# Decoder trunk with routed experts on one core: gate folded from the second quarter, one block more combined on TensorE, the scatter buffer read back in one load

## The chip, the cores and the metric

The kernel runs on one core of one Trainium2 chip. The metric is the device time of one execution in microseconds (us). The kernel before was run three times: median 2093.63 us, 2091.58 to 2093.67. One more execution was recorded by the profiler; it took 2093.2 us. Engine names are those of the profile: PE is TensorE, DVE is VectorE, ACT is ScalarE, POOL is GpSimd, SP is the engine that issues most weight loads.

## The reference

The reference is a two-layer decoder trunk on 512 tokens of width 1024, in float32. For each of four sub-layers (mixer 0, experts 0, mixer 1, experts 1) it computes

```python
h = x * (1 + scale) + shift                 # scale, shift, gate: rows made from the vector c
x = layer_norm(ALPHA * x + gate * f(h), g, b)   # ALPHA = 4 ** 0.25
```

Here f is in layer 0 a mixer of block-sparse attention and gated linear attention with one joint output projection (1024 x 1024), in layer 1 a gated delta-rule mixer with an output projection of the same size, and behind each mixer a layer of 64 experts (width 256) with one shared expert. Each token goes to 6 experts, chosen through groups; the sum is weighted by the router and scaled by 2.5.

## The kernel before, in words

**Tiles and stages.** The 512 tokens are four tiles of 128; x is kept as four tiles of 128 x 1024 floats. The span of 2091.1 us falls into layer 0's mixer (to about 381 us, with its output projection from about 283), the experts of layer 0 (to 995), layer 1's mixer (to about 1450, projection from about 1360), the experts of layer 1 (to 2065) and a tail of LayerNorm.

**Float32 by three products.** A weight slab or activation is split in a high part (ACT copies it rounded, L217) and a low part (DVE subtracts, L219), into one of two `parts` buffers; each product is three matmuls: high x high, high x low, low x high (L231, L232, L233).

**Output projection (`out_project`).** The weight is read in four quarters of 256 columns, w0 to w3, through a ring of three slots. Quarters below `FOLD` are multiplied plain, and DVE multiplies the result by the gate row `grow` (L399, into `op`) and adds it to x (L401). From `FOLD` on, POOL multiplies the weight in its slot by the gate row (L385, 128 x 2048), it is split behind that, and DVE adds PE's result directly. w0 and w1 are one step each; w2 and w3 are one step together, since the result then fills 512 columns. POOL first scales x by ALPHA (L377, four instructions). x is loaded before that.

**Rows.** A row of the gate or of LayerNorm is made by PE transposes of a broadcast column (L279) in two halves of 512 columns, which ACT copies out of PSUM (L281).

**Experts.** 64 experts stand in 38 blocks: 20 blocks of one expert, 14 of two, 4 of four. One pass of the loop, number b, holds the down projection of block b - 1 (`narrow`, L1368), gate and up projection of block b (`widen`, L1335), then transposes of the gathered tokens of block b + 1 (`turn`, L1323), two transposes of block b's hidden rows (`turn_back`, L1346), and small matmuls that find a later block's token slots (L1269). The result of a block of one is added to a buffer in DRAM, `acc`, by an indirect DMA of POOL's queue (L1375). The result of a shared block is split in `yh` and `yl` and added to x by `combine`: eight units (four token tiles, two halves), each two matmuls with a one-hot matrix into one of three `ps_tr` buffers (L1395) and one add by DVE (L1396). Behind the loop stands another loop, for experts with more tokens than their block holds; all engines meet at its head (L1711).

**Order.** In the expert loop PE's order is the order of the program. Elsewhere, and for the other engines, a scheduler orders each engine's instructions when the program is built; each engine then runs its own list in order.

## Time and profile before

| | |
|---|---|
| median of three runs | 2093.63 us |
| the profiled execution | 2093.2 us, span 2091.1 us |
| mean granted TensorE clock | 0.971 |
| PE busy | 1935.5 us, 93% |
| DVE busy | 1234.7 us, 59% |
| ACT, POOL busy | 507.1 us, 24%; 453.8 us, 22% |

The span is the time from the first to the last instruction that the profile shows. The busy time of PE is that of its matmuls; weight loads run beside them. A row of a timeline gives start, length, engine, line, operation, what it writes and reads; in brackets, the idle time of that engine just before it and what ended it. Rows of equal instructions in a run stand as one with x and their count.

### The profile page before, as it was taken

What the parts mean: (1) busy time and instruction counts of PE and PEld (TensorE: products, weight loads), DVE (VectorE), ACT (ScalarE), POOL (GpSimd) and SP (SyncE); (2) the same over time, 40 slices, a digit from 0 to 9 for tenths busy, and PEclk for the clock granted to TensorE, in tenths of its full rate; (3) what the DMA queues carried; (4) which work ended last, traced back from release to release, by engine and by line L of the source; (5) the groups of instructions that cost most, each with busy time, mean ns of one, the idle gap of its engine ahead of it and who ended that gap; (6) DMA issues with size and microseconds to landing.
All of it is one profiled execution on the core that took longest, in us unless ns stands there. A gap on an engine that the chain in (4) does not pass through costs nothing. (4 is left out here: it accounts for less than half of the span.)

```text
span 2091.1 us, 28643 instructions
## 1 busy us (share of the span) xinstructions
PE 1935.5 (93%) x10619; PEld 1189.4 (57%) x10619; DVE 1234.7 (59%) x3165; ACT 507.1 (24%) x969; POOL 453.8 (22%) x317
## 2 busy tenths in 40 slices
PE   5999879999999999998888999989999999999995
PEld 3877779644444444543676877888544444444442
DVE  6676887743553544535768877578453544544436
ACT  3412443111111111111434556423111111111111
POOL 2331234311011110111125344154211110110102
PEclk9999999999999999999889999999999999999997
DMA  8765665898998998988322112128898989989994
GB/s 308 274 235 206 219 215 212 299 362 318 411 386 330 401 353 345 400 338 320 114 72 81 41 42 67 42 106 313 323 353 345 397 312 406 371 331 399 396 359 143
DMA packets 128678, 572.17 MB, mean 274 GB/s; under 512 B 16943, under 2 KB 54255, under 8 KB 72473
## 3 DMA queue, kind: packets, MB, share of 16 engines
q1 hardware_dynamic: 103600, 499.81, 60.8%
q0 software_dynamic: 19632, 55.79, 9.5%
q10 hardware_dynamic: 5304, 14.72, 1.9%
q8 instruction: 85, 1.39, 0.3%
q14 instruction: 57, 0.46, 0.1%
HBM read 550.33 MB, written 34.61 MB: 280 GB/s over the span
## 5 line engine op out<-in xcount | busy, mean ns | idle before, releaser
L1335 PE MATMUL ps_mm<-wslot,xT 128*64 128x512 f32 (+2 forms) x1216 | 404.5, 596 | 1.2 <-ACT xT L1324 0.8
L1368 PE MATMUL ps_mm<-wslot,hT 128*64 128x512 f32 (+2 forms) x1024 | 312.8, 610 | 0.2
L1335 PE MATMUL ps_mm<-parts,xT 128*64 128x512 f32 (+2 forms) x832 | 280.0, 596 | 0.7 <-issue 0.4
L1335 PEld LDWEIGHTS ps_mm<-wslot,xT 128*64 128x64 f32 (+2 forms) x1216 | 142.1, 148 | 219.1 <-issue 205.4
L1337 DVE SCALAR_TENSOR_TENSOR hh<-hh,t,ps_mm 128x256 f32<-128x256 f32 x76 | 36.5, 480 | 360.2 <-ACT hh L1336 360.1
L1293 POOL DMA_INDIRECT xg<-hd,idx x76 | 93.5, 1230 | 579.6 <-PE ps_tr L1395 497.0
L231 PE MATMUL ps_mm<-parts,hTh 128*128 128x256 f32 x704 | 208.9, 298 | 9.4 <-DVE op L399 5.3
L1368 PEld LDWEIGHTS ps_mm<-wslot,hT 128*64 128x64 f32 (+2 forms) x1024 | 103.1, 149 | 189.9 <-issue 179.9
L232 PE MATMUL ps_mm<-parts,hTh 128*128 128x256 f32 x704 | 204.1, 291 | 0.7 <-DVE parts L219 0.4
L233 PE MATMUL ps_mm<-parts,hTl 128*128 128x256 f32 x704 | 203.5, 291 | 0.4 <-DVE hTl L1773 0.4
L1396 DVE TENSOR_TENSOR x<-x,ps_tr 128x512 f32<-128x512 f32 x288 | 183.6, 681 | 5.8 <-PE ps_tr L1395 5.1
L224 POOL TENSOR_TENSOR parts<-wslot,parts 128x512 fp32r<-128x512 f32 (+1 forms) x79 | 140.9, 1809 | 194.6 <-ACT parts L217 194.6
L1336 ACT ACTIVATE hh<-ps_mm 128x256 f32<-128x256 f32 x76 | 29.1, 383 | 619.9 <-PE ps_mm L1335 619.9
L1375 POOL DMA_INDIRECT acc<-yh,row x40 | 64.9, 1622 | 489.4 <-DVE yh L1374 480.0
L1335 PEld LDWEIGHTS ps_mm<-parts,xT 128*64 128x64 f32 (+2 forms) x832 | 93.7, 144 | 130.4 <-issue 123.2
L1395 PE MATMUL ps_tr<-yh,ohs 128*128 128x512 f32 x288 | 137.7, 478 | 26.2 <-DVEq L1711 14.1
L231 PEld LDWEIGHTS ps_mm<-parts,hTh 128*128 128x128 f32 x704 | 138.5, 197 | 13.0 <-DVE op L399 3.2
L1324 ACT ACTIVATE xT<-ps_tr 128x512 f32<-128x512 f32 x152 | 84.0, 597 | 245.7 <-PE ps_tr L1323 245.7
L232 PEld LDWEIGHTS ps_mm<-parts,hTh 128*128 128x128 f32 x704 | 138.3, 197 | 3.3 <-issue 1.3
L233 PEld LDWEIGHTS ps_mm<-parts,hTl 128*128 128x128 f32 x704 | 137.5, 196 | 1.7 <-DVE hTl L1773 0.6
L255 DVE SCALAR_TENSOR_TENSOR acc<-wslot,cact,acc 128x2048 f32<-128x2048 f32 x38 | 122.7, 3230 | 13.6 <-DMA wslot<-in_ada_w_dram 13.2
L231 PE MATMUL ps_mm<-hTh,parts 128*128 128x512 f32 (+1 forms) x296 | 124.2, 419 | 4.8 <-ACT parts L217 2.5
(457 smaller groups left out, 3114.9 us busy)
## 6 DMA issues: line engine op xcount, KB each, us to landing
wslot<-in_moe_w_down_dram SPq DMA_DIRECT2D x128, 1024.0 KB
wslot<-in_moe_w_gate_dram SPq DMA_DIRECT2D x76, 1024.0 KB
wslot<-in_moe_w_up_dram SPq DMA_DIRECT2D x76, 1024.0 KB
parts<-in_moe_w_gate_dram SPq DMA_DIRECT2D x52, 1024.0 KB
parts<-in_moe_w_up_dram SPq DMA_DIRECT2D x52, 1024.0 KB
wslot<-in_ada_w_dram SPq DMA_DIRECT2D x44, 1024.0 KB
wslot<-in_od_w_in_dram SPq DMA_DIRECT2D x16, 1024.0 KB
wslot<-in_ev_w_in_dram SPq DMA_DIRECT2D x12, 1024.0 KB
```

The lines of the kernel that those rows point to most:

```text
L224: eng.tensor_sub(lo[:, ks], v[:, ks], hi[:, ks].bitcast(F32))
L231: self.nc.tensor.matmul(out, ah, bh, start=(i == 0), stop=False)
L232: self.nc.tensor.matmul(out, ah, bl, start=False, stop=False)
L233: self.nc.tensor.matmul(out, al, bh, start=False, stop=(i == n - 1))
L255: nc.vector.scalar_tensor_tensor(acc, w, self.cact[:, k:k + 1], acc, op0=OP.mult, op1=OP.add)
L1293: self.nc.gpsimd.indirect_dma_start(out=xg, out_offset=None, in_=M["hd"], in_offset=bass.IndirectOffsetOnAxis(ap=idx, axis=0), bounds_chec ...
L1324: nc.scalar.activation(xT[:, 4 * g:4 * g + 4], pt.rearrange("p (k c) -> p k c", k=4), AF.Copy)
L1335: nc.tensor.matmul(pv[a:a + n], xT[:, i, a:a + n], w[0][:, :, i], start=(i == 0), stop=(i == KT - 1))
L1368: nc.tensor.matmul(py[a:a + n], hT[:, k, a:a + n], w[1][:, k, 512 * h:512 * h + 512], start=(k == 0), stop=(k == 1))
L1375: nc.gpsimd.indirect_dma_start(out=M["acc"], out_offset=bass.IndirectOffsetOnAxis(ap=G["tok"], axis=0), in_=yf, in_offset=None, bounds_che ...
L1395: nc.tensor.matmul(po, G["oh"][:, t], y[:, cs], start=(i + k == 0), stop=(i == len(Gs) - 1 and k == 1))
L1396: nc.vector.tensor_add(self.x[t][:, cs], self.x[t][:, cs], po)
```

## The change

- `FOLD` goes from 2 to 1: the gate is folded in the weights of w1, w2 and w3, in both layers.
- In layer 0's mixer the second half of the gate row and of the two LayerNorm rows is copied out of PSUM by DVE (`both`).
- A block of one is added to `acc` only if it is not among the last four blocks (`stored`). This concerns block 35, which now goes through `combine` at iteration 36.
- `acc` is read back by one DMA of 2 MB at iteration 35, into a slot of the expert weights, and added to x by four POOL instructions at iteration 36. Before, eight DMAs of 256 KB and eight DVE adds stood at iteration 37 (L1636, L1637).
- In an iteration with `combine`, all eight units stand behind turn, slots and turn_back. Before, four stood ahead of them and four behind.
- The second half of `route_extra`, which makes the table of the extra experts, moves from iteration 4 to iteration 5.

```diff
--- before.py
+++ after.py
@@ -34,7 +34,7 @@
 NX = 1
 EARLY = 4
 LEAD = 3
-FOLD = 2
+FOLD = 1
 LANES = 64
 ALPHA = float(4 ** 0.25)
 LN_EPS = 1e-5
@@ -68,6 +68,13 @@
 
 
 BLOCKS = blocks()
+
+
+def stored(b):
+
+    return len(BLOCKS[b]) == 1 and b < len(BLOCKS) - 4
+
+
 SPE = (mybir.EngineType.SP,)
 
 
@@ -270,7 +277,7 @@
             nc.vector.tensor_add(m, m, b)
         return end
 
-    def row(self, out, col, scale=1.0):
+    def row(self, out, col, scale=1.0, both=False):
 
         for h in range(2):
             pt = self.ptile("tr")
@@ -278,7 +285,10 @@
                 kk = 4 * h + k
                 self.nc.tensor.transpose(pt[:, k * P:(k + 1) * P], col[:, kk:kk + 1].to_broadcast([P, P]),
                                          self.ident)
-            self.nc.scalar.activation(out[:, h * 512:(h + 1) * 512], pt, AF.Copy, scale=scale)
+            if both and h:
+                self.nc.vector.tensor_copy(out[:, h * 512:(h + 1) * 512], pt)
+            else:
+                self.nc.scalar.activation(out[:, h * 512:(h + 1) * 512], pt, AF.Copy, scale=scale)
 
     def rows_here(self, new, which, l, scale=1.0):
 
@@ -288,7 +298,7 @@
             self.row(t[k], self.lncol[:, 2 * which + k, l, :], scale)
         return t
 
-    def rows_next(self, new, which, l, nxt):
+    def rows_next(self, new, which, l, nxt, both=False):
 
         nc = self.nc
         g, b = self.lncol[:, 2 * which, l, :], self.lncol[:, 2 * which + 1, l, :]
@@ -300,7 +310,7 @@
         t = []
         for k in range(2):
             t.append(new("lnrow"))
-            self.row(t[k], cg[:, k])
+            self.row(t[k], cg[:, k], both=both)
         return t
 
     def ln_stats(self, x):
@@ -1238,6 +1248,7 @@
         nc.vector.tensor_scalar(oh[:, 2], ex[:, :E], xcol, -1.0, op0=OP.subtract, op1=OP.mult)
         nc.vector.scalar_tensor_tensor(oh[:, 2], oh[:, 2], 1.0, oh[:, 0], op0=OP.add, op1=OP.mult)
         nc.vector.tensor_reduce(lst, oh[:, 1:3], axis=X, op=OP.add)
+        yield
         pl = self.ptile("sm")
         for k in range(2):
             nc.tensor.matmul(pl[:, L * k:L * k + L], lst[:, k:k + 1].to_broadcast([L, P]),
@@ -1496,8 +1507,8 @@
         def slots():
 
             if nsl[0] < NB:
-                b = BLOCKS[nsl[0]]
-                g = self.slots_of(M, M["posm"], M["vals"], [x[0] for x in b], len(b) == 1)
+                b = nsl[0]
+                g = self.slots_of(M, M["posm"], M["vals"], [x[0] for x in BLOCKS[b]], stored(b))
                 nsl[0] += 1
                 yield next(g)
                 at.append(next(g))
@@ -1532,7 +1543,7 @@
 
             for b in range(NB + 1):
                 n = len(BLOCKS[b - 1]) if b > SINGLE else 0
-                first = n if n == 2 else n // 2
+                first = n if n == 2 or n == 1 and not stored(b - 1) else n // 2
                 yield from down(b - 1, range(first))
                 if b < NB:
                     yield from wide(b)
@@ -1598,7 +1609,7 @@
                     else:
                         fetch(total)
                     if b < NB:
-                        G[b]["w"], G[b]["one"] = W[b], len(W[b]) == 1
+                        G[b]["w"], G[b]["one"] = W[b], stored(b)
                         row.append(self.widen(M, G[b]))
                     if not todo:
                         row.reverse()
@@ -1610,31 +1621,29 @@
                     if todo and b < NB:
                         units = [lambda g=todo, t=t, h=h: self.combine(g, t, h) for t in range(TT) for h in range(2)]
                         todo = []
-                    for u in units[:4]:
-                        u()
                     if b + 1 < NB:
                         ahead()
                     if b < NB and not units:
                         self.turn_back(M, G[b])
                     if b + 1 < NB:
                         self.turn(M, G[b + 1])
+                    next(sl, None)
                     if b < NB and units:
                         self.turn_back(M, G[b])
-                    next(sl, None)
-                    for u in units[4:]:
+                    for u in units:
                         u()
                     units = []
                     if b == NB - 3 and pre:
                         pre(False)
                     if b == NB - 1 and pre:
                         pre(True)
-                    if b == NB - 1:
+                    if b == NB - 3:
+
+                        back = self.eslot(M).rearrange("p (t d) -> p t d", t=TT)
+                        nc.gpsimd.dma_start(back, M["acc"][:S].rearrange("(t p) d -> p t d", p=P))
+                    if b == NB - 2:
                         for t in range(TT):
-                            for h in range(2):
-                                cs = slice(512 * h, 512 * h + 512)
-                                y = self.wk("acc")
-                                nc.gpsimd.dma_start(y, M["acc"][t * P:(t + 1) * P, cs])
-                                nc.vector.tensor_add(self.x[t][:, cs], self.x[t][:, cs], y)
+                            nc.gpsimd.tensor_add(self.x[t], self.x[t], back[:, t])
                     if b == NB - 8:
                         wds = [wd[:, 1], wd[:, 0]]
                         new = lambda n: wds.pop()
@@ -1643,7 +1652,11 @@
                         for t in range(TT):
                             self.ln_here(self.x[t], M["mv"][t], here, nc.vector, nc.vector)
                     if b == 4:
-                        self.route_extra(M)
+                        rest = self.route_extra(M)
+                        next(rest)
+                    if b == 5:
+                        for _ in rest:
+                            pass
                         for k in range(2):
                             nc.vector.tensor_mul(wd[:, k], wd[:, k], grow)
                     if 8 <= b < 24 and b % 2 == 0:
@@ -1826,8 +1839,8 @@
             grow = new("grow")
             while len(todo) > 2:
                 fill(1)
-            self.row(grow, self.mod[:, 0, 2])
-            rows = self.rows_next(new, 0, 0, (self.mod[:, 0, 3], self.mod[:, 0, 4]))
+            self.row(grow, self.mod[:, 0, 2], both=True)
+            rows = self.rows_next(new, 0, 0, (self.mod[:, 0, 3], self.mod[:, 0, 4]), True)
             wr = self.router(0, new)
             self.out_project(mixed, d["ev_w_out"][0], grow, d["x"][0], fill, (0, 1, 4, 5, 6, 7, 2, 3))
             while todo or queue:
```

Lines below the change move: L385 becomes L395, L399 and L401 become L409 and L411, L219 and L217 become L226 and L224, L231 to L233 become L238 to L240, L1335 and L1368 become L1346 and L1379, L1395 becomes L1406, L1230 and L1243 become L1240 and L1254, L1323 becomes L1334, L1346 (turn_back) becomes L1357, L1269 becomes L1280.

On DVE, in layer 1's output projection, the list before reads so from the split of w2 (L219, first row) to the first sum of w2 and w3 (last row); the split of w1 stands 12 rows ahead of the first gate multiply and is not in the piece.

```order
L219 TENSOR_TENSOR parts<-wslot,parts 128x2048
L399 TENSOR_TENSOR op<-ps_mm,grow 128x256
L401 TENSOR_TENSOR x<-x,op 128x256
L311 BN_STATS bn<-x 128x6
L399 TENSOR_TENSOR op<-ps_mm,grow 128x256
L401 TENSOR_TENSOR x<-x,op 128x256
L311 BN_STATS bn<-x 128x6
L399 TENSOR_TENSOR op<-ps_mm,grow 128x256
L401 TENSOR_TENSOR x<-x,op 128x256
L311 BN_STATS bn<-x 128x6
L219 TENSOR_TENSOR parts<-wslot,parts 128x2048
L401 TENSOR_TENSOR x<-x,ps_mm 128x512
```

The same place now, from the splits of w1 and w2 (L226 x2) on:

```order
L226 TENSOR_TENSOR parts<-wslot,parts 128x2048 x2
L411 TENSOR_TENSOR x<-x,ps_mm 128x256
L321 BN_STATS bn<-x 128x6
L411 TENSOR_TENSOR x<-x,ps_mm 128x256
L321 BN_STATS bn<-x 128x6
L411 TENSOR_TENSOR x<-x,ps_mm 128x256
L321 BN_STATS bn<-x 128x6
L411 TENSOR_TENSOR x<-x,ps_mm 128x256
L321 BN_STATS bn<-x 128x6
L226 TENSOR_TENSOR parts<-wslot,parts 128x2048
L411 TENSOR_TENSOR x<-x,ps_mm 128x512
```

The split of w1 moved to behind quarter 0's adds, next to that of w2, and the four gate multiplies of quarter 1 (L399) are gone. On POOL the four scalings of x (L387) are followed by three gatings (L395) where there were two, and on ACT the three splits (L224) stand in one run.

On PE, in iteration 4 of the first expert loop, the table of the extra experts (L1230, L1231, L1243) stands so ahead of the down projection (L1368):

```order
L1230 LDWEIGHTS rx
L1230 MATMUL ps_sm<-supper_b,rx 64x64
L1231 LDWEIGHTS rx
L1231 MATMUL ps_sm<-upper_b,rx 64x64
L1243 MATMUL ps_sm<-call,rx 128x64 x2
L1368 MATMUL ps_mm<-wslot,hT 64x512 x8
```

and now:

```order
L1240 LDWEIGHTS rx
L1240 MATMUL ps_sm<-supper_b,rx 64x64
L1241 LDWEIGHTS rx
L1241 MATMUL ps_sm<-upper_b,rx 64x64
L1379 MATMUL ps_mm<-wslot,hT 64x512 x8
```

The two matmuls L1243 (now L1254) went to iteration 5, behind the combine.

On PE, in iteration 5, from the last of widen (first row), before:

```order
L1335 MATMUL ps_mm<-wslot_3688,xT 128x512 x8
L1395 MATMUL ps_tr<-yh,ohs 128x512
L1395 MATMUL ps_tr<-yl,ohs 128x512
L1395 MATMUL ps_tr<-yh,ohs 128x512
L1395 MATMUL ps_tr<-yl,ohs 128x512
L1395 MATMUL ps_tr<-yh,ohs 128x512
L1395 MATMUL ps_tr<-yl,ohs 128x512
L1395 MATMUL ps_tr<-yh,ohs 128x512
L1395 MATMUL ps_tr<-yl,ohs 128x512
L1323 MATMUL ps_tr<-call,xg_2910 128x128 x8
L1346 MATMUL ps_sm<-call,hh 128x128 x2
```

and now:

```order
L1346 MATMUL ps_mm<-wslot_3681,xT 128x512 x8
L1334 MATMUL ps_tr<-call,xg_2903 128x128 x8
L1280 LDWEIGHTS oh
L1280 MATMUL ps_sm<-tb,oh 128x5
L1280 LDWEIGHTS oh
L1280 MATMUL ps_sm<-tb,oh 128x5
L1280 LDWEIGHTS oh
L1280 MATMUL ps_sm<-tb,oh 128x5
L1280 LDWEIGHTS oh
L1280 MATMUL ps_sm<-tb,oh 128x5
L1357 MATMUL ps_sm<-call,hh 128x128 x2
L1406 MATMUL ps_tr<-yh,ohs 128x512
```

All units (L1406) begin behind turn (L1334), the slots (L1280) and turn_back (L1357).

## Rows read from the trace of the kernel before

**Rows 1.** The profile page, part 1: busy time of each engine (us, share, instructions).

```profile
PE 1935.5 (93%) x10619; PEld 1189.4 (57%) x10619; DVE 1234.7 (59%) x3165; ACT 507.1 (24%) x969; POOL 453.8 (22%) x317
```

**Rows 2.** What TensorE waited for: us in total, times, longest.

```profile
PE ps_tr L1395 <- DVEq L1711: 14.1, 2, 8.0
PE ps_tr L1395 <- DVE x L1396: 12.1, 30, 4.0
...
PE ps_mm L231 <- DVE op L399: 5.3, 2, 3.0
PE ps_sm L1243 <- DVE rx L1240: 4.6, 2, 2.3
```

**Rows 3.** Timeline of POOL, layer 1's out_project: start us, us, instruction [idle before <-releaser].

```profile
1369.08 9.37 POOL L385 TENSOR_TENSOR wslot<-wslot,grow 128x2048 f32<-128x2048 f32 x2
```

**Rows 4.** Timeline of ACT, the same stretch.

```profile
1373.72 1.92 ACT L217 ACTIVATE parts<-wslot 128x2048 fp32r<-128x2048 f32 x1 [13.48 <-POOL wslot L385]
1379.84 1.91 ACT L217 ACTIVATE parts<-wslot 128x2048 fp32r<-128x2048 f32 x1 [4.19 <-PE ps_mm L233]
```

**Rows 5.** Timeline of DVE, the same stretch.

```profile
1368.52 0.42 DVE L399 TENSOR_TENSOR op<-ps_mm,grow 128x256 f32<-128x256 f32 x1 [0.31 <-PE ps_mm L233]
1369.15 4.82 DVE L401 TENSOR_TENSOR x<-x,op 128x256 f32<-128x256 f32 x1 [0.21 <-POOL x L377]
...
1379.38 2.27 DVE L219 TENSOR_TENSOR parts<-wslot,parts 128x2048 fp32r<-128x2048 f32 x1
...
1391.46 0.69 DVE L401 TENSOR_TENSOR x<-x,ps_mm 128x512 f32<-128x512 f32 x1 [3.07 <-PE ps_mm L233]
```

**Rows 6.** Timeline of POOL, layer 0's out_project.

```profile
293.58 11.17 POOL L385 TENSOR_TENSOR wslot<-wslot,grow 128x2048 f32<-128x2048 f32 x2
```

**Rows 7.** Timeline of DVE, layer 0's out_project.

```profile
293.65 6.69 DVE L255 SCALAR_TENSOR_TENSOR acc<-wslot,cact,acc 128x2048 f32<-128x2048 f32 x1 [2.07 <-DMA wslot<-in_ada_w_dram]
...
320.38 0.69 DVE L401 TENSOR_TENSOR x<-x,ps_mm 128x512 f32<-128x512 f32 x1 [2.43 <-PE ps_mm L233]
```

**Rows 8.** Timeline of ACT, layer 0's out_project.

```profile
309.32 1.91 ACT L217 ACTIVATE parts<-wslot 128x2048 fp32r<-128x2048 f32 x1 [9.19 <-PE ps_mm L233]
```

**Rows 9.** Timeline of PE, iteration 4 of the first expert loop.

```profile
445.42 1.11 PE L1243 MATMUL ps_sm<-call,rx 64*128 64x64 f32 x4 [2.29 <-DVE rx L1240]
446.47 5.32 PE L1368 MATMUL ps_mm<-wslot,hT 128*64 128x512 f32 x16
```

**Rows 10.** A window around that row: PE PEld DVE ACT POOL busy, PEclk, DMA share, GB/s.

```profile
446.00:452.00 6.00, 6.00 (x20) 2.05 (x20) 1.72 (x5) 0.63 (x1) 0.08 (x1) 0.68 0.75 221
```

**Rows 11.** Timeline of PE, an iteration with a block of two experts.

```profile
558.27 0.40 PE L1395 MATMUL ps_tr<-yh,ohs 128*128 128x512 f32 x1
...
558.74 0.39 PE L1395 MATMUL ps_tr<-yh,ohs 128*128 128x512 f32 x1
...
559.56 0.50 PE L1395 MATMUL ps_tr<-yh,ohs 128*128 128x512 f32 x1 [0.20 <-DVE x L1396]
```

**Rows 12.** Timeline of DVE, the same iteration.

```profile
558.82 2.48 DVE L1396 TENSOR_TENSOR x<-x,ps_tr 128x512 f32<-128x512 f32 x4
```

**Rows 13.** Timeline of PE, an iteration with a block of four.

```profile
660.95 0.50 PE L1395 MATMUL ps_tr<-yl,ohs 128*128 128x512 f32 x1 [0.98 <-DVE yl L1384]
```

**Rows 14.** Timeline of PE, the end of the first expert loop.

```profile
978.18 0.50 PE L1395 MATMUL ps_tr<-yh,ohs 128*128 128x512 f32 x1
...
983.22 3.65 PE L1368 MATMUL ps_mm<-wslot,hT 128*64 128x512 f32 x16
994.90 0.80 PE L1395 MATMUL ps_tr<-yh,ohs 128*128 128x512 f32 x1 [8.02 <-DVEq L1711]
```

**Rows 15.** Timeline of DVE, the end of the first expert loop.

```profile
986.42 3.09 DVE L1637 TENSOR_TENSOR x<-x,acc 128x512 f32<-128x512 f32 x5
...
993.19 0.68 DVE L1382 TENSOR_TENSOR y<-ps_mm,grow 128x512 f32<-128x512 f32 x1
```

**Rows 16.** DMA issues: KB each, us to landing.

```profile
acc<-xg POOLq DMA_DIRECT2D x2, 2560.0 KB, 16.0
```

## Prediction

> **What bounds the kernel now.** Read part 1 of the page first: TensorE (PE) is busy in 93% of the span [rows 1]. So a change can pay only by shortening PE's waits, by letting PE run at its full clock, or by giving PE less to do. The second view is the list of what PE waited for. The change touches these rows of it: 14.1 us for VectorE (DVE) to reach the loop behind the experts, 12.1 us for the adds of the combine, 5.3 us for the gate multiply of the output projection, 4.6 us for the extra experts' table; the waits on yl are read from a timeline [rows 2, 13]. Together the four are near 36 us, less than 2% of the span. The rest of the views are timelines of the stretches where those waits stand: the output projection of each mixer, one iteration of the expert loop for each kind of block, and the loop's end.
>
> The sum is made against the profiled execution, 2093.2 us (span 2091.1); the median of the runs is 2093.63.
>
> **1. Gate folded from the second quarter: layer 1.** Before, quarter 1 (w1) was split early, so PE ran it straight behind quarter 0: quarter 0's last result came at 1368.5, and ScalarE (ACT) got w1's buffer back at 1379.8, so quarter 1 took 11.3 us [rows 4, 5]. POOL gated w2 and w3 in that shadow, from 1369.1, 4.7 us each [rows 3]. Now w1 itself stands at the head of that queue, behind the same four scalings of x, and ACT's split of it behind the gating: 1369.1 + 4.7 = 1373.8, + 1.9 for ACT [rows 4] = 1375.7. Then DVE must make the low half, 2.27 us alone [rows 5]. But DVE's add with both operands in SBUF took 4.82 us beside the gating, and ended when POOL's instruction did [rows 3, 5]; the multiply of the same size ahead of it took 0.42. So I let DVE's split of w1 wait for POOL's second instruction, till 1378.5, and end at 1380.7. PE stands idle from 1368.5: 12.2 us with nothing to cover it, where it had none. Quarter 1 then runs till 1392.0, and at half clock at first. A long wait before costs about 1.7: behind a 2.29 us wait the same 16 matmuls took 5.32 instead of 3.65, at a mean granted clock of 0.68, a mix of the levels 1.2 and 2.4 GHz [rows 9, 10, 14]. That gives 1393.7. w3 needs w1's buffer, so it is split behind that (1.9 + 2.3, 1397.9), hidden by two tiles of w2 (48 of quarter 1's 96 matmuls, 5.6 us, till 1399.3). The first sum lands 2.9 us later, at 1402.2; before it landed at 1391.5 [rows 5]: +10.7. The gate wait of the last row (5.3 - 3.0 = 2.3 us, [rows 2]) is gone within this. Off goes what the early split of w1 no longer takes from ACT and DVE ahead of the projection, at most 1.9 (ACT's copy). I take **+8.5**. Bounds: DVE not held up (-2.8), no half clock (-1.7): +4; a gating of quarter 1 held up in its turn by DVE: +12.
>
> The Trainium skill ("SBUF — State Buffer", section "SBUF: two separate sides") says that DVE with two SBUF inputs and a reading GpSimd take a shared port pair as an exclusive lock, held for the whole instruction, not as a split of bandwidth. The 4.82 agrees. With a split of bandwidth the low half of w1 would be done at about 1378 to 1379, and the sum would fall by about 2 per layer.
>
> **2. The same in layer 0.** POOL gates from 293.6, 11.17/2 = 5.6 us an instruction with DVE against it, 4.7 without [rows 6]. w1 is gated at 298.2, split by ACT at 300.1, by DVE behind w2's gating at about 305. Before, quarter 1 ended at 309.3 [rows 8], in spite of a 3.0 us wait in its middle, for DVE was held by a modulation step of 6.69 us [rows 2, 7]; that wait goes, since that step now stands behind the splits. Quarter 1 now ends at 305 + 11.3 + 1.7 = 318, which is +8.7. The last two modulation slabs are loaded only when w1's and w2's slots are free (305 and 309.6): they are worked off just before 318, so they are hidden, and cost up to 4 if that cover fails. The halves of the LayerNorm rows copied by DVE are 3 copies of about 0.7 (as the last DVE row of [rows 5], the same size) behind its scaling of mixed, and ACT's three copies less and one split less bring the rows 1 to 2 earlier. I take **+6.5** for the layer; bounds +3 to +10.
>
> **3. The extra experts' table in two halves.** The second half moves to iteration 5, behind the combine. Twice PE waited 2.3 for it [rows 2, 9]; and the half-clock matmuls behind it go. 2 x (2.3 + 1.7) = **-8**. Bounds -4.6 (the clock falls elsewhere) to -8.5. DVE has a whole iteration for those steps, about 16 us (983.2 - 446.5 over 33 iterations, [rows 9, 14]), so nothing is late next.
>
> **4. Eight combine units in one piece.** Of the 18 shared blocks per layer, four are fours. There PE waits 0.98 for yl [rows 13]; turn, slots and turn_back now stand ahead and cover it, but the later adds bunch up: -0.4 each, **-3** in all. For the 14 twos, the two groups of four with a rest between become eight in a row. DVE's adds come every 0.62 (2.48/4, [rows 12]), PE's units, undisturbed, every 0.47 (558.27 to 558.74, [rows 11]), and there are three ps_tr buffers: unit 8 cannot begin before add 5 is done. Before, the same iteration lost 0.20 in one wait [rows 11]. Now: add 1 starts 0.6 behind unit 1, five adds take 3.1, so unit 8 begins 3.7 behind unit 1 where PE alone wants 3.3: 0.4 lost, 0.1 to 0.2 more than before. 28 of these, 0.15 each: **+4**; bounds -7 to +7, for DVE's small copies may fall on either side of the adds.
>
> **5. Block 35 combined, the buffer back in one load.** Iteration 36 gets eight units more, 5.0 us in the last iteration, 978.18 to 983.22 [rows 14]: +4.5 per layer, PE time with no cover. What goes: eight DVE adds, 8 x 0.62, which stand between narrow's end and the last scaling of y (986.4 to 993.2, [rows 15]), and the waits on eight loads among them. PE waited 8.0 and 6.1 there [rows 2, 14]. Without the adds the y scaling follows narrow's end at once, and what is left is ACT's and DVE's split and the loop's entry, some 3 us: 5 and 3 off. Net about **+1** for both layers; bounds -4 to +5. The load of 2 MB is bounded by the 2.5 MB load's 16.0 us [rows 16] and is issued in iteration 35; POOL's four adds of about 2.4 each follow, and the next combine that needs x stands one iteration later. So both are hidden, by about 3 us; a load slower by 5 would show as 2 us per layer.
>
> By the page named above, a DVE add that takes one operand from PSUM is not held by that lock, so POOL's four adds would not slow the combine beside them; no run so far shows that pair. If they did, up to 4 x 2.4 per layer would come on top.
>
> **Sum:** 8.5 + 6.5 - 8 - 3 + 4 + 1 = +9, that is 2102.2 against the profiled run, 2102.6 against the median.
>
> **The rivals.**
> *Gains win (faster, about 2086).* Quarter 1 is late by less than the waits it removes. POOL's gating of w1 starts sooner, or DVE's split gets between POOL's instructions: with the low bounds of terms 1 and 2 (+4, +3), the waits on the loop's entry falling to 2 each (-10 in place of -8 in term 5, so -1), -8, -4, and 0 for the twos: -6 to -8. For it: the early split of w1 also cost ACT and DVE time ahead of the projection, and no row shows three gatings in a row. Against: POOL's queue has the scalings first, and the one row of DVE beside a gating is a full wait. Chance 0.24.
> *No change (about 2093).* Terms 1 and 2 at +5 each, the rest as summed to -6, -3 for twos that gain instead of lose. Chance 0.17.
> *A larger loss (about 2112).* The place is the end of both loops. If the load back comes later than the next combine, POOL's adds hold DVE's, and those PE's units: from 3 us of lateness on, each us counts in both layers; with terms 1 and 2 at their upper bounds (+22) and this at +3, the sum is +18 to +20. Chance 0.15; the forecast itself 0.44.
>
> **Chances.** A measurement of this kernel can't tell 0.2% (4.2 us) from no change. Slower by more: the forecast and the larger loss, 0.59. Same 0.17, faster 0.24. The range for 8 in 10: 2086 to 2114. The forecast's own is 2097 to 2108.
>
> **What would show it.** Right: in layer 1 PE idle for 10 us or more ahead of quarter 1, ended by DVE's split of w1, and that split's start or its length tied to the end of POOL's second gating; the first sum of quarters 2 and 3 8 to 11 us later behind the last of quarter 0; no wait on rx, and full clock in iteration 4; the wait for the loop's entry down to about 3. Wrong: quarter 1 starting less than 5 us behind quarter 0, the twos' iterations shorter than before by over 0.2 us, or PE waiting on x in the last combine.

## The result, and the profile after

The changed kernel took 2110.06 us (median of 3 runs, 2106.03 to 2112.76) against 2093.63; the ratio is 1.0076, with an interval of 1.0059 to 1.0094, that is 12 to 20 us slower. Its profiled execution took 2112.76 us, with a span of 2110.8, the longest of its three runs: what follows explains 19.7 us of span, not the 16 of the medians.

Where they came from is read from the same PE instruction in both timelines, the first transposes for a block of the expert loop (L1323 before, L1334 after). The shift of its start, after minus before:

| stretch | shift at its end, us | of which here |
|---|---|---|
| layer 0's mixer, to the transposes for block 0 | 7.8 | +7.8 |
| experts of layer 0, to the transposes for block 37 | 8.6 | +0.8 |
| last iterations, second loop, layer 1's mixer | 17.7 | +9.1 |
| experts of layer 1, to the transposes for block 37 | 17.6 | -0.1 |
| last iterations, second loop, tail | 19.7 | +2.0 |

These are single executions. Of the +7.8 of the first row, up to 2.9 can be chance: e3_route below, which changes nothing ahead of that point, is 2.9 us late there too.

The waits of PE after (total us, times, longest) show the trade. PE's old rows on op and on rx [rows 2] are gone, the wait for the second loop fell from 14.1 to 5.1; new on top stand the two halves of a split weight:

```profile
PE ps_mm L238 <- ACT parts L224: 17.1, 3, 7.4
...
PE ps_mm L239 <- DVE parts L226: 8.0, 3, 3.9
PE ps_tr L1406 <- DVE x L1407: 8.0, 5, 3.5
...
PE ps_tr L1406 <- DVEq L1724: 5.1, 2, 2.9
```

**The projection of layer 1.** POOL's timeline after, which answers to [rows 3], has three gatings in a row:

```profile
1376.93 15.71 POOL L395 TENSOR_TENSOR wslot<-wslot,grow 128x2048 f32<-128x2048 f32 x3
```

ACT's, against [rows 4]; the splits of w1, w2 and w3:

```profile
1381.45 1.91 ACT L224 ACTIVATE parts<-wslot 128x2048 fp32r<-128x2048 f32 x1 [13.63 <-POOL wslot L395]
1386.11 1.91 ACT L224 ACTIVATE parts<-wslot 128x2048 fp32r<-128x2048 f32 x1 [2.75 <-POOL wslot L395]
1401.81 1.92 ACT L224 ACTIVATE parts<-wslot 128x2048 fp32r<-128x2048 f32 x1 [13.79 <-PE ps_mm L240]
```

DVE's, against [rows 5]: quarter 0's last multiply and add, the low halves of w1 and w2 in one row, the first sum of w2 and w3:

```profile
1376.10 0.42 DVE L409 TENSOR_TENSOR op<-ps_mm,grow 128x256 f32<-128x256 f32 x1
1376.99 4.71 DVE L411 TENSOR_TENSOR x<-x,op 128x256 f32<-128x256 f32 x1 [0.47 <-POOL x L387]
1383.39 11.40 DVE L226 TENSOR_TENSOR parts<-wslot,parts 128x2048 fp32r<-128x2048 f32 x2 [1.69 <-ACT parts L224]
...
1409.11 0.69 DVE L411 TENSOR_TENSOR x<-x,ps_mm 128x512 f32<-128x512 f32 x1 [3.06 <-PE ps_mm L240]
```

And PE's, from the stretch where it had one wait of 2.4 us before:

```profile
1383.41 1.01 PE L238 MATMUL ps_mm<-parts,hTh 128*128 128x256 f32 x3 [7.35 <-ACT parts L224]
1388.28 0.58 PE L239 MATMUL ps_mm<-parts,hTh 128*128 128x256 f32 x1 [3.86 <-DVE parts L226]
```

ACT copies w1 as soon as POOL has gated it (1381.45), PE begins quarter 1 with the high half (wait of 7.35) and stops after three matmuls for the low half (3.86). Quarter 1 then starts at the lower level of the clock: the granted clock was 0.50 in 1388 to 1393 us and 0.99 in 1393 to 1399. DVE's row of 11.40 us is two instructions of 2.27: the first ends at 1388.2, behind POOL's second gating (1376.93 + 2 x 4.6 = 1386.1) by its own length, the second behind the third gating. From quarter 0's last multiply to the first sum of the last two quarters it is now 33.0 us (1376.10 to 1409.11); before it was 22.9 (1368.52 to 1391.46).

**The experts.** In iteration 4 the wait on rx is gone in both layers, but in layer 0 the matmuls behind it still run at half clock in part (5.35 us, as long as with the wait), against [rows 9, 10]; PE's timeline, and a window with the granted clock in the third number from the end:

```profile
450.85 5.35 PE L1379 MATMUL ps_mm<-wslot,hT 128*64 128x512 f32 x16
```

```profile
450.00:456.00 6.00, 5.93 (x22) 1.95 (x22) 4.64 (x27) 0.63 (x1) 1.45 (x2) 0.72 1.02 360
```

So layer 0 gained 2.6 us there, layer 1 5.3. An iteration with a block of four, against [rows 13], from the yh that the first unit waits for to the next iteration's first matmuls:

```profile
668.96 0.51 PE L1406 MATMUL ps_tr<-yh,ohs 128*128 128x512 f32 x1 [0.39 <-ACT yh L1394]
669.68 0.50 PE L1406 MATMUL ps_tr<-yl,ohs 128*128 128x512 f32 x1 [0.22 <-DVE yl L1395]
...
674.78 1.51 PE L1346 MATMUL ps_mm<-wslot,xT 128*64 128x512 f32 x6
```

and DVE in it:

```profile
670.93 0.68 DVE L1407 TENSOR_TENSOR x<-x,ps_tr 128x512 f32<-128x512 f32 x1
...
671.59 4.26 DVE L1407 TENSOR_TENSOR x<-x,ps_tr 128x512 f32<-128x512 f32 x7
```

Eight adds follow each other, from 670.93 to 675.8, and PE has only units to run beside them: 0.61 us longer in this iteration than before. For a block of two the difference is 0.02. Behind the transposes for block 13, in both layers, another row is new: the granted clock was 0.57 in 584 to 588 us, a mix of its two levels, and the down projection there took 4.18 us, where 3.63 is usual:

```profile
583.43 3.08 PE L1457 MATMUL ps_mm<-wd,sh 128*128 128x512 f32 x4
586.44 4.18 PE L1379 MATMUL ps_mm<-wslot,hT 128*64 128x512 f32 x16
```

That cost 1.65 us in each layer. A third stretch of the kind, 1.6 us, stands behind the transposes for block 31 of layer 1 (granted clock 0.66 in 1959 to 1964 us): sixteen transposes took 3.23 us for 1.97 before, and the row behind them, 3.65 before, took 3.99:

```profile
1962.40 3.99 PE L1379 MATMUL ps_mm<-wslot,hT 128*64 128x512 f32 x16
```

Ahead of all three PE had run sixteen small matmuls of the slots (128 x 5) with waits under 0.3 us. The kernel before has the same run ahead of its full-clock row behind block 31, so these matmuls alone do not decide it.

**The end of the loop.** DVE and PE, against [rows 14, 15]:

```profile
982.12 6.02 DVE L1397 TENSOR_SCALAR ohs<-call,t 128x128 fp32r<-128x128 f32 x3
```

```profile
992.65 0.50 PE L1357 MATMUL ps_sm<-call,hh 128*128 128x128 f32 x2 [1.00 <-DVE hh L1348]
...
1004.06 1.33 PE L1406 MATMUL ps_tr<-yh,ohs 128*128 128x512 f32 x2 [2.87 <-DVEq L1724]
```

PE's wait for the second loop fell from 8.02 to 2.87 us in layer 0, which pays for the eight units there. DVE's three one-hot tiles, 0.67 us in the iteration before, took 6.02, since POOL was adding (978.70 to 988.05). The load itself landed in time:

```profile
wslot<-acc POOLq DMA_DIRECT2D x2, 2048.0 KB, 19.4
```

### The profile page after: what moved, and what is told of

It is laid out like the page before. It is cut to its first block, busy times and chain, and to the rows that moved or that the text cites. A ratio compares the mean times of both kernels' runs of the same rounds, so it can differ in the third digit from the quotient of the medians.

```text
span 2110.8 us, 28677 instructions
## 1 busy us (share of the span) xinstructions
PE 1955.9 (93%) x10651; PEld 1189.3 (56%) x10651; DVE 1250.1 (59%) x3170; ACT 507.9 (24%) x971; POOL 474.8 (22%) x311
## 5 line engine op out<-in xcount | busy, mean ns | idle before, releaser
L1346 PE MATMUL ps_mm<-wslot,xT 128*64 128x512 f32 (+2 forms) x1216 | 404.5, 596 | 1.2 <-ACT xT L1335 1.0
L1379 PE MATMUL ps_mm<-wslot,hT 128*64 128x512 f32 (+2 forms) x1024 | 311.0, 606 | 0.1
L1346 PE MATMUL ps_mm<-parts,xT 128*64 128x512 f32 (+2 forms) x832 | 279.9, 596 | 1.0 <-ACT xT L1335 0.7
L1346 PEld LDWEIGHTS ps_mm<-wslot,xT 128*64 128x64 f32 (+2 forms) x1216 | 142.1, 148 | 219.8 <-issue 205.4
L238 PE MATMUL ps_mm<-parts,hTh 128*128 128x256 f32 x704 | 207.8, 298 | 17.6 <-ACT parts L224 14.6
L1379 PEld LDWEIGHTS ps_mm<-wslot,hT 128*64 128x64 f32 (+2 forms) x1024 | 102.6, 148 | 189.4 <-issue 178.3
L240 PE MATMUL ps_mm<-parts,hTl 128*128 128x256 f32 x704 | 203.5, 291 | 0.0
L231 POOL TENSOR_TENSOR parts<-wslot,parts 128x512 fp32r<-128x512 f32 (+1 forms) x79 | 141.3, 1815 | 195.8 <-ACT parts L224 185.5
L1346 PEld LDWEIGHTS ps_mm<-parts,xT 128*64 128x64 f32 (+2 forms) x832 | 92.8, 144 | 131.0 <-issue 122.7
L1406 PE MATMUL ps_tr<-yh,ohs 128*128 128x512 f32 x304 | 146.1, 482 | 17.0 <-DVE x L1407 8.0
L238 PEld LDWEIGHTS ps_mm<-parts,hTh 128*128 128x128 f32 x704 | 138.0, 197 | 21.3 <-ACT parts L224 15.0
L240 PEld LDWEIGHTS ps_mm<-parts,hTl 128*128 128x128 f32 x704 | 137.9, 197 | 1.0 <-DVE hTl L361 0.2
L1335 ACT ACTIVATE xT<-ps_tr 128x512 f32<-128x512 f32 x152 | 83.4, 595 | 188.0 <-PE ps_tr L1334 185.3
L1406 PE MATMUL ps_tr<-yl,ohs 128*128 128x512 f32 x304 | 124.7, 412 | 3.6 <-DVE yl L1395 3.6
L238 PE MATMUL ps_mm<-hTh,parts 128*128 128x512 f32 (+1 forms) x296 | 123.4, 417 | 4.8 <-ACT parts L224 2.5
```

The source lines that it names most:

```text
L231: eng.tensor_sub(lo[:, ks], v[:, ks], hi[:, ks].bitcast(F32))
L238: self.nc.tensor.matmul(out, ah, bh, start=(i == 0), stop=False)
L240: self.nc.tensor.matmul(out, al, bh, start=False, stop=(i == n - 1))
L1335: nc.scalar.activation(xT[:, 4 * g:4 * g + 4], pt.rearrange("p (k c) -> p k c", k=4), AF.Copy)
L1346: nc.tensor.matmul(pv[a:a + n], xT[:, i, a:a + n], w[0][:, :, i], start=(i == 0), stop=(i == KT - 1))
L1379: nc.tensor.matmul(py[a:a + n], hT[:, k, a:a + n], w[1][:, k, 512 * h:512 * h + 512], start=(k == 0), stop=(k == 1))
```

## The experiments

Each kernel was run in five rounds beside the kernel before; differences in us are worked out from the ratio of the runs times 2094.

**e1_fold2.** The changed kernel with one line back:

```diff
-FOLD = 1
+FOLD = 2
```

> The changed kernel with FOLD = 2 again; all its other parts stay. Theory (the fold costs about 8 us in each projection, for quarter 1 waits for gating, split and the lock between POOL and DVE): the two waits of 7.3 and 3.9 us ahead of quarter 1 go in both layers, and the time falls by 16 us against the changed kernel, to about +0 to +4 against the kernel before. Rival (the loss is made in the expert loop, by the combine in one piece and the load back; the projection's waits are made good later): the time falls by less than 5 us, and the kernel stays above +11 against before.

Measured: ratio 1.0006 (0.9997 to 1.0016), +1 us against before, 15 less than the changed kernel. The fold carries the loss: in its profile the two waits on the halves of w1 are gone in both layers.

**e2_fold1.** The kernel before with the opposite edit.

> The kernel before with FOLD = 1 and nothing else. Theory: +16 us (7.8 in layer 0, 8.2 in layer 1), with the waits ahead of quarter 1 as in the changed kernel. Rival: below +5 us.

Measured: 1.0061 (1.0046 to 1.0077), +13 us. The transposes' shift is 7.7 us behind layer 0's mixer and 6.9 more behind layer 1's. PE's waits ahead of quarter 1 in layer 1 are 6.30 and 3.86 us. POOL's gatings, DVE's splits and the first sum of w2 and w3 are much as in the changed kernel:

```profile
1374.16 15.91 POOL L385 TENSOR_TENSOR wslot<-wslot,grow 128x2048 f32<-128x2048 f32 x3
```

```profile
1380.81 11.41 DVE L219 TENSOR_TENSOR parts<-wslot,parts 128x2048 fp32r<-128x2048 f32 x2 [1.69 <-ACT parts L217]
...
1406.08 0.69 DVE L401 TENSOR_TENSOR x<-x,ps_mm 128x512 f32<-128x512 f32 x1 [3.06 <-PE ps_mm L233]
```

**e3_route.** The table in two halves alone (two multiplies by the gate row go to iteration 5 with it):

```diff
+        yield
...
-                        self.route_extra(M)
+                        rest = self.route_extra(M)
+                        next(rest)
+                    if b == 5:
+                        for _ in rest:
+                            pass
```

> The kernel before with the extra experts' table alone in two halves (iterations 4 and 5). Theory: the two waits of 2.3 us on rx go, and the half-clock matmuls behind them, together -8 us. Rival (the half clock falls on another stretch, since the expert loop has such waits elsewhere): -4.6 us or less, with the down projection of iteration 4 still at 5.2 us instead of 3.6.

Measured: 0.9955 (0.9940 to 0.9970), -9 us. Here the down projection of iteration 4 is at full clock:

```profile
445.92 3.65 PE L1369 MATMUL ps_mm<-wslot,hT 128*64 128x512 f32 x16
```

The two iterations gave 4.5 and 5.5 us, layer 1's at full clock too. But the rival came in part as well: 1.6 us were lost again behind the transposes for block 31 of layer 1, where the kernel before had full clock (0.79 in 1934 to 1942 us; before, 1.00 in 1940 to 1948):

```profile
1937.99 4.60 PE L1369 MATMUL ps_mm<-wslot,hT 128*64 128x512 f32 x16
```

That the half clock comes of the wait on rx is not shown. The changed kernel lost the wait and kept the half clock in layer 0. In e5_back, e8_backpc and e11_rows, which keep the wait, layer 1's matmuls of iteration 4 took 4.96 to 5.17 us for the 6.33 of the kernel before, and the stretch behind block 31 is there too.

**e4_comb.** The combine's order alone:

```diff
-                    for u in units[:4]:
-                        u()
...
-                    for u in units[4:]:
+                    for u in units:
                         u()
```

with `next(sl, None)` ahead of `turn_back`.

> The kernel before with the combine's eight units in one piece behind turn, slots and turn_back, nothing else. Theory now, read from the changed kernel's iterations: +0.6 us for each of 8 blocks of four, nothing for the twos: +5 us. What the prediction had: -3 for the fours, +4 for the twos: +1 us.

Measured: 1.0035 (1.0022 to 1.0049), +7 us. In its profile 5.9 stand inside the two expert loops: 4.1 in the blocks of four (0.6 each in six of the eight, 0.25 each in the last of either layer), 1.6 in a stretch behind the transposes for block 23 of layer 0 (granted clock 0.78 in 742.4 to 750 us), little in the twos. Of the rest, 2.2 stand behind the last transposes of layer 1: 1.4 in a longer wait for the second loop (7.49 us for 6.04), 0.8 in the last iteration. That one has no transposes, so turn_back, now first, waits for hh:

```profile
2057.57 0.50 PE L1346 MATMUL ps_sm<-call,hh 128*128 128x128 f32 x2 [0.99 <-DVE hh L1337]
```

The prediction's +1 is out.

**e5_back.** Block 35 combined, one load, four POOL adds, alone.

```diff
...
+                    if b == NB - 3:
+                        back = self.eslot(M).rearrange("p (t d) -> p t d", t=TT)
+                        nc.gpsimd.dma_start(back, M["acc"][:S].rearrange("(t p) d -> p t d", p=P))
+                    if b == NB - 2:
+                        for t in range(TT):
+                            nc.gpsimd.tensor_add(self.x[t], self.x[t], back[:, t])
...
```

> The kernel before with block 35 combined, the buffer read back in one load at iteration 35 and added by four POOL instructions at iteration 36; nothing else. Theory: the eight units more cost about 4.5 us a layer, the wait for the loop's entry falls by 5 and 3 us, and POOL's adds, while they run, hold DVE's making of the one-hot tiles (6.0 us for three where 0.67 is usual), which delays hh by about 1 us a layer: +2 to +4 us in all. What the prediction had: +1, with POOL's adds hidden.

Measured: 0.9995 (0.9984 to 1.0007), -1 us: nothing that can be told from zero, and less than expected. The one-hot tiles are held up here too, three of them 4.90 us, while the combine's four adds ahead of them, with one operand in PSUM, keep their 0.62 (POOL adds from 968.98 to 978.4):

```profile
971.17 2.48 DVE L1401 TENSOR_TENSOR x<-x,ps_tr 128x512 f32<-128x512 f32 x4 [0.22 <-PE ps_tr L1400]
973.57 4.90 DVE L1391 TENSOR_SCALAR ohs<-call,t 128x128 fp32r<-128x128 f32 x3
```

but hh is not late, and PE has no wait of 1.0 us on it. So that wait of the changed kernel is not POOL's doing: it comes of turn_back ahead of the units, as e4_comb's 0.99, without any POOL adds, shows. My expectation put the two together wrongly.

**e8_backpc.** The same with POOL's adds in sixteen pieces of 128 x 256.

> The same as e5_back, with POOL's four adds of 128 x 1024 cut in sixteen of 128 x 256. If DVE waits for a POOL instruction to end, as a lock for whole instructions would have it, each one-hot tile now waits 0.6 us at most, the three take under 3 us, and the wait on hh at the end of iteration 37 (1.0 us a layer) goes: -2 us against e5_back. If POOL and DVE share by bandwidth, the three tiles stay near 6 us and nothing is gained.

Measured: 0.9990 (0.9977 to 1.0003), -2 us, not told apart from e5_back. DVE beside POOL's pieces:

```profile
973.11 1.84 DVE L1391 TENSOR_SCALAR ohs<-call,t 128x128 fp32r<-128x128 f32 x3
...
975.47 0.85 DVE L1391 TENSOR_SCALAR ohs<-call,t 128x128 fp32r<-128x128 f32 x1
976.24 1.23 DVE L1389 TENSOR_TENSOR yl<-y,yh 128x512 fp32r<-128x512 f32 x1
```

Three one-hot tiles took 1.84, one took 0.85 (0.27 usual), a yl of 0.69 took 1.23: each waits for about the rest of one piece. Waits went with the length of POOL's instruction, as a lock per instruction has it; the time did not. The gain of 2 us that was expected rested on the wait on hh, which e5_back had not.

**e10_pieces.** The fold alone, each gating in four pieces of two k-steps.

```diff
+                for k in range(0, KT, 2):
+                    self.tc.keep_in_program_order(nc.gpsimd.tensor_mul(w[:, k:k + 2], w[:, k:k + 2], ...))
```

> The kernel before with FOLD = 1, the gating in the same place as in the changed kernel but each quarter cut in four POOL instructions of 128 x 512. Theory of a lock held for one instruction: DVE's split of w1 starts within 1.2 us of ACT's copy instead of at the end of w2's gating: -2.5 us a layer against the fold alone (+13), so about +8 against before. If the hold-up came of shared bandwidth, or of something else that POOL's whole run of gatings does, it stays at +13.

Measured: 1.0042 (1.0025 to 1.0060), +9 us. DVE's split of w1 no longer waits for w2's gating:

```profile
1379.53 2.62 DVE L219 TENSOR_TENSOR parts<-wslot,parts 128x2048 fp32r<-128x2048 f32 x1 [5.54 <-ACT parts L217]
```

PE's second wait ahead of quarter 1 is 1.65 us instead of 3.86. The first, for the gating and ACT's copy, stays: 7.53 us, and 6.30 in e2_fold1, where POOL began 0.8 us earlier against quarter 0 and one gating was 0.4 shorter than four pieces.

```profile
1379.55 1.01 PE L231 MATMUL ps_mm<-parts,hTh 128*128 128x256 f32 x3 [7.53 <-ACT parts L217]
1382.21 0.58 PE L232 MATMUL ps_mm<-parts,hTh 128*128 128x256 f32 x1 [1.65 <-DVE parts L219]
```

```profile
1402.59 0.69 DVE L406 TENSOR_TENSOR x<-x,ps_mm 128x512 f32<-128x512 f32 x1 [3.10 <-PE ps_mm L233]
```

From POOL's first gating (1372.45, shown at the end) to the first sum of w2 and w3 it is 30.1 us, in e2_fold1 31.9; in layer 0 the difference is 1.2. So by the timelines the hold-up is worth 1.2 to 1.8 us a layer, not the 2.5 expected; by the ratios it is 4 of 13 us, with overlapping intervals. Either way it is the smaller part of the loss. That w1's place in POOL's queue is the larger is tried next.

**e7_early.** The same, with w0 and w1 loaded first and w1 gated ahead of the scalings of x.

```diff
...
+        early = {q: gated(q) for q in range(2)}
         self.x = []
...
```

> The kernel before with FOLD = 1, where w0 and w1 are loaded first and POOL gates w1 (in four pieces) ahead of the scalings of x; w2 and w3 are gated in four pieces each behind them. Theory (what costs in the fold is w1's place behind the scalings in POOL's queue): quarter 1 follows quarter 0 with a wait under 2 us, the gate multiplies of quarter 1 are gone and with them the waits of 3.0 and 2.4 us: -3 to -6 us against before, against +13 for the fold alone. Rival (the gating itself, or the load of w1's slab, is late wherever it stands): +5 us or more.

Measured: 1.0050 (1.0030 to 1.0070), +10 us. The expectation failed, though its premise held: PE's waits ahead of quarter 1 are gone in layer 1 (1.2 us for w2 and 1.4 for w3 come later). There the loss moved to the transposes ahead of quarter 0. POOL, DVE and PE in layer 1:

```profile
1356.69 5.09 POOL L379 TENSOR_TENSOR wslot<-wslot,grow 128x512 f32<-128x512 f32 x4
```

```profile
1354.35 1.14 DVE L658 SCALAR_TENSOR_TENSOR mixed<-mixed,ss,gate 128x128 f32<-128x128 f32 x4 [1.18 <-POOL ss L239]
...
1356.76 5.17 DVE L658 SCALAR_TENSOR_TENSOR mixed<-mixed,ss,gate 128x128 f32<-128x128 f32 x4 [0.59 <-POOL ss L239]
```

```profile
1362.59 1.12 PE L370 MATMUL ps_tr<-call,mixed 128*128 128x128 f32 x4 [4.65 <-DVE hTl L372]
```

DVE's four scalings of mixed took 1.14 us in the first group and 5.17 beside POOL's four pieces: one piece of 1.3 us each. PE's transposes of mixed waited 4.65 for DVE's next copy behind it. In layer 0 the loop starts 4.6 us late, and PE waits 4.72 us in the projection for a modulation step (1.98 before); what that comes from was not tried.

**e9_dep.** e7_early with POOL's gating tied to the end of those scalings:

```diff
...
+        late = self.wk("op")[:, :256]
+        nc.vector.scalar_tensor_tensor(late, mixed[TT - 1][:, D - 256:], 0.0, grow[:, 256:512], op0=OP.mult, op1=OP.add)
...
```

> As e7_early (FOLD = 1 on the kernel before, w1 gated ahead of the scalings of x), but the gate row for w1 is taken from a copy that DVE makes from it plus zero times the last tile of mixed, so that POOL's gating of w1 begins behind DVE's scaling of mixed. Theory (in e7_early quarter 1 no longer waits, and what is left of the loss is DVE's scaling of mixed, 5.2 us beside POOL's gating where 1.1 is usual, each of its four instructions waiting for one of POOL's): the wait of 4.7 us ahead of the transposes of mixed falls under 1.5 in layer 1; layer 1's mixer falls from +3.5 to about 0 or below against before, and the time by 4 to 7 us against e7_early, to about +4. Rival (those waits come from the load of w1 holding a ring slot): less than 2 us.

Measured: 1.0006 (0.9997 to 1.0016), +1 us, 9 less than e7_early, more than the 4 to 7 expected. The scalings are short again, and POOL follows:

```profile
1352.23 1.14 DVE L660 SCALAR_TENSOR_TENSOR mixed<-mixed,ss,gate 128x128 f32<-128x128 f32 x4 [0.59 <-POOL ss L239]
```

```profile
1354.38 5.00 POOL L381 TENSOR_TENSOR wslot<-wslot,op 128x512 f32<-128x512 f32 x4 [2.19 <-DVE op L367]
```

Layer 1's mixer is 3.3 us shorter than before, layer 0's 1.0 longer; 1.3 of the 3.3 lie in layer 0's second loop, where e3_route and e11_rows, which change nothing there, have them too. What remains is a wait of 3.25 us, for ACT's copies of hTh stand behind its split of w1:

```profile
1361.86 0.38 PE L231 MATMUL ps_mm<-parts,hTh 128*128 128x256 f32 x1 [3.25 <-ACT hTh L373]
```

**e11_rows.** The halves of the rows copied by DVE, alone (`both=True` at layer 0's gate row and LayerNorm rows).

> The kernel before with the second halves of layer 0's gate and LayerNorm rows copied by DVE, nothing else. Theory: the copies stand behind DVE's scaling of mixed, PE gets its ps_tr buffers back 1 to 2 us later or as before: 0 to +2 us, seen in layer 0's mixer alone. Rival (the copies relieve ACT and shorten its wait of 3.3 us on grow): -2 us.

Measured: 1.0014 (1.0004 to 1.0024), +3 us. But in its profile the transposes behind layer 0's mixer are 0.2 us late, and the profiled execution took 2093.13 us, where the median of its runs is 2095.58. Where 3 us would be is not seen; it stays open.

**e12_best.** The kernel before with e3's and e8's edits.

> The kernel before with the extra experts' table in two halves and block 35 combined, the buffer read back in one load and added by POOL in sixteen pieces; FOLD stays 2, the combine's order and the rows stay. If the parts add up: -9.5 from the table and -2 from the load, about 2082 us. If the half clock moves with the loop's timing, only part of the table's gain stays: 2085 to 2088.

Measured: 0.9964 (0.9951 to 0.9977), -8 us, median 2085.14: the second case of the expectation, not the sum of the parts. The half clock did move. In its profile layer 0's matmuls of iteration 4 are at half clock in part without any wait on rx (granted clock 0.72 in 442 to 448 us), and the 1.6 us behind block 31 of layer 1 are there:

```profile
443.72 5.35 PE L1374 MATMUL ps_mm<-wslot,hT 128*64 128x512 f32 x16
```

The load adds nothing to the table's gain that these runs could tell.

**e13_fold1late.** e12_best with layer 1's fold as in e9_dep, and ACT's split of w1 pinned behind its copies of hTh.

> e12_best, and in layer 1 alone w1's gate folded as in e9_dep (gated in four pieces behind DVE's scaling of mixed and ahead of the scalings of x, w2 and w3 in four pieces each), with ACT's split of w1 behind its copies of hTh. In e9_dep layer 1's mixer was 3.3 us shorter than before, in spite of a wait of 3.25 us on hTh that came from that split standing between the copies. If the waits are what the fold is worth, this is 3 to 5 us less than e12_best, about 2081 us; if w1's low half, which now stands behind quarter 0's adds on DVE, comes as late as the wait that it removes, it stays within 1 us of e12_best.

Measured: 0.9951 (0.9937 to 0.9964), -10 us, median 2084.22: the lowest ratio of all that were run, not told apart from e12_best (the intervals overlap). The wait on hTh is gone, but w1's low half is now late by 2.25:

```profile
1366.63 0.39 PE L240 MATMUL ps_mm<-parts,hTh 128*128 128x256 f32 x1 [2.25 <-DVE parts L227]
...
1376.71 0.39 PE L239 MATMUL ps_mm<-parts,hTh 128*128 128x256 f32 x1 [1.50 <-DVE x L422]
```

The medians are 0.9 us apart, the ratios 2.7, so the runs exclude neither of its two cases. The trace shows what the second names: one late operand took the place of another. Its profile also has full clock in iteration 4 of both layers and behind block 31, which e12_best's has not, so a gain over e12_best could be the clock's.

## Why the prediction was right, and where it was not

It forecast slower, 2102.6 us in a range of 2086 to 2114; measured were 2110.06. The side and its main cause, the fold, were right. The sum was short by 7.5 us: the result lies outside the 2097 to 2108 that the forecast calls its own, near the 2112 of the larger loss, whose reason (a late load) did not occur.

- *Layer 1's fold (+8.5).* Right. The first sum came 10.1 us later behind quarter 0, where +10.7 was worked out. Ahead of it 1.0 us was saved (1.7 in e2_fold1), where up to 1.9 was taken, so the row of the table is +9.1. Quarter 1 began at half clock, as said. DVE's split ended 2.2 us behind POOL's second gating, as the step said. What it left out: PE starts on the high half as soon as ACT has it, and so waits twice (7.35 and 3.86). The step had 2.8 of its 10.7 for the lock; e10_pieces against e2_fold1 shows 1.8 in layer 1.
- *Layer 0's fold (+6.5).* Right within what can be read: +7.8 in the changed kernel, +7.7 in e2_fold1, on a start of the loop that itself shifted by 2.9 us in e3_route, which changes nothing ahead of it.
- *The table (-8).* The time is right, -9 alone, and the waits on rx went. The reason for the other part, that the half clock stands behind that wait, is not borne out: the changed kernel and e12_best lost the wait and kept 5.35 us for the matmuls in layer 0 (only 2.6 of 4 came there), while e3_route has full clock in iteration 4 and a new slow stretch elsewhere. That the time came out as summed has some luck in it.
- *The combine in one piece (+1).* This step failed. "Turn, slots and turn_back now stand ahead and cover it" was said of yl's wait, and those waits did shrink (0.39, 0.22 and 0.23 for 0.98 before). But the same instructions had been the cover for the first four adds. With all adds behind them, PE's units run at DVE's pace: the fours lose about 0.6 each where -0.4 was taken, the twos 0.02 where +0.15 was. The last iteration of each loop, where turn_back has no transposes to cover hh, waits 1 us more. Alone it is +7, not +1, and that is most of what the sum lacked; of the +7, the 1.6 us at half clock in e4_comb's profile are not explained by this.
- *Block 35 and the load (+1).* Right as a sum: -1 alone, with an interval from -3 to +1. The load took 19.4 us for 2 MB, more than the bound of 16.0 that was read from the 2.5 MB row, and was still hidden. POOL's adds did hold DVE, though not at the combine's adds but at the one-hot tiles; it cost no time that e8_backpc could show.
- *Not foreseen:* the half clock behind the transposes for block 13, 1.65 us in each layer, and for block 31 of layer 1, 1.6, in a profile of one execution. Stretches behind block 13 or 23 stand only in the three kernels with the combine in one piece (this one, e1_fold2, e4_comb); why is open. The single edits sum to 13 - 9 + 7 - 1 + 3 = +13, within the 12 to 20 of the whole; the runs cannot say how much the clock adds.

## What to carry to other kernels

An operand that is moved from a plain load to a chain of POOL, ACT and DVE must be followed from the head of POOL's queue: here it was needed when POOL began to gate it, and PE waited for the gating, ACT's copy and DVE's split. Moving it ahead (e7_early) stops the loss only once DVE's work with two SBUF operands is out of its way (e9_dep). Before a producer's work is gathered in one run, ask what it ran beside: the transposes between two groups of adds were their cover. Two edits that each take away a wait can leave one late operand in its place, so look at each wait's successor. And a gain from the clock, read in one execution behind one wait, should not be put down to that wait until a kernel without it has shown so.

## What the runs showed of the hardware

DVE instructions with one SBUF operand and a scalar column (the one-hot tiles, 128 x 128) were held up by POOL's additions as fully as those with two operands: three took 4.90 us in e5_back, where three usually take 0.67. The prediction had weighed the hold-up only for two operands. An add with one operand in PSUM was not held: e5_back's took 0.62 us each beside POOL's adds. The Trainium skill ("SBUF — State Buffer", section "Who interferes with whom") says that a DVE instruction with at most one SBUF input, outside the two-port modes, does not contend with GpSimd; these adds agree. With POOL's work in pieces, DVE got in after about one piece each time. The hold-up goes both ways: ten of e10_pieces' twelve pieces took 1.26 to 1.44 us and two, beside DVE's splits, 3.3, which makes 19.11 us, where the three whole gatings of the changed kernel took 15.71 (4.49, 4.69 and, beside a split, 6.60):

```profile
1372.45 19.11 POOL L386 TENSOR_TENSOR wslot<-wslot,grow 128x512 f32<-128x512 f32 x12
```
